# Gates projected beside the scans and stored, and all the memory's keys beside the first convolutions: a hybrid encoder layer

## The chip, the cores and the metric

The kernel runs on one core of a Trainium2 chip. The metric is the device time of one execution in microseconds. The kernel before took 1302.97 us, the median of three runs (1302.38 to 1303.3). All numbers below are from one profiled execution of it.

## The reference, cut to what matters

One layer over 512 tokens of width 1024, in float32:

```python
h = rms_norm(x)
z, xBC, dt_f, dt_b, q, k, v, gates = split(h @ w_in)
xBC = silu(conv5(xBC))                    # centred, depthwise
y = ssd_scan(forward) + ssd_scan(backward) + d_skip * xs   # 4 groups of 8 heads
branch_ssd  = group_rmsnorm(y * silu(z)) @ w_branch_ssd
branch_attn = windowed_attention(rope(q), rope(k), v) @ w_branch_attn
g_ssd, g_attn = sigmoid(gates)            # 1024 columns each
x = x + (g_ssd * branch_ssd + g_attn * branch_attn) @ w_out
x = x + cross_attention(rms_norm(x), rms_norm(mem))    # mem: 256 tokens; keys and values from mem
x = x + swiglu_ffn(rms_norm(x))
return rms_norm(x)
```

The change concerns two projections: the gates of the attention branch (`g_attn`, 8 tiles of 128 columns of `h @ w_in`) and the keys of the memory (8 tiles of 128 columns of `mem_n @ w_kv`).

## The kernel before, in words

Data lie transposed, 128 columns on the partitions and tokens along the free axis, so a projection's result is a tile of 128 x 512 (128 x 256 for the memory). Each matrix product is done in three passes: an operand is split into a high part (`hh`, `whi`) and a low remainder (`hl`, `wlo`), and `mac` (L134 to L141) issues for each of 8 slices hi x hi (L139), hi x lo (L140) and lo x hi (L141): 24 matmuls, accumulated in one PSUM bank of the tag "mm", of which there are three.

A weight tile of 512 KB ("granule") is fetched by SP into `raw` (L121, two buffers), cast by ScalarE into `whi` (L129) and subtracted by VectorE into `wlo` (L130), three buffers each. The program is a list of `steps`, and each granule is loaded LOOK = 2 granules ahead of its step.

The stages: values and keys of the memory and the first norm; the dt step and the first group's convolutions; four group scans; the attention branch; the merge of the two branches; cross-attention; feed-forward. In the first part, up to the attention branch, a planner orders the instructions of each engine by a simulated timeline; the step list gives the priorities. Each engine then works through its own order strictly, waiting where something is late. Later stages are ordered by priority too, so that matmuls of a following step fill in among earlier ones.

A convolution (`conv`, L406 to L417) empties its bank by one ScalarE activation and four VectorE multiply-adds (L414). A group's scan (`group_scan`) has weighing on POOL into `xw` (L495, two buffers), carried states (L503 to L510), decay rows fetched by SP (`rt`), masked on POOL (L537) and exponentiated on ScalarE (L544), added on POOL (L550), multiplied on VectorE (L555), and the inner products on TensorE (L565). Beside a scan the kernel weaves other projections, in an order written by hand in the strings `ONE` and `TWO`: "m" the next group's convolutions, "z" its own z, "o" the output projection of the group before. The first group has no group before it; its "o" slots take five of the eight memory keys. The other three keys are woven with the first group's convolutions (KV1 = 11 of the 16 steps of `kv`; the first eight are values).

A key (`mem_k`, L257 to L262) is scaled by VectorE into an `xw` buffer and stored in DRAM by a DMA that POOL issues; a value (`mem_v`) likewise, from ScalarE. The memory's normalised tiles use the buffers of `vh` and `vl`, which each group's normalised output needs.

In the merge, for each of 8 tiles: `gate_a` projects the gate from `hh`, `hl` and takes a tanh into `ta` (L871, two buffers), then `branch_a` projects the attention output, VectorE multiplies by the gate (L879) and adds the other branch (L880), and the result is split into `mh`, `ml`. The merge's buffers lie where attention's lay, so `ta` and `xr` (x read again, L898) can be written only when attention is through. The gates of the other branch, `gate_s`, are projected in the last scan and in attention.

Of the kernel before, what the change touches and what calls it, by code (L numbers as in the profile page):

```python
# [9 lines left out]
F32 = mybir.dt.float32  # L10
F32R = mybir.dt.float32r
AF = mybir.ActivationFunctionType
# [3 lines left out]
P = 128  # L16
D = 1024
S = 512
KT = D // P
# [21 lines left out]
G_DT, G_K, G_V, G_Q, G_GA, G_SSD, G_GS, G_N = 0, 1, 3, 5, 13, 21, 61, 69  # L41
LOOK = 2
KV0 = 8
G0, G1, TL = 2, 3, 2
KV1 = 11
RB = 3
MB = 3
SPLIT = 1
# [3 lines left out]
HALF = 1  # L52
KVB = 2
LO_POOL = range(0)
HI_DVE = range(79, 89)
ZP = 2
ONE = "mrwomomoo"
TWO = "mzmzm"
LAST = "zezee"
LAG1, LAG2, LAG3 = 1, 2, 5  # L60
# [5 lines left out]
def weave(a, b):  # L66

    key = [((i + 0.5) / len(a), 0, i) for i in range(len(a))] + [((i + 0.5) / len(b), 1, i) for i in range(len(b))]
    return [(a, b)[w][i] for _, w, i in sorted(key)]
# [3 lines left out]
def bidir_hybrid_layer(ctx: ExitStack, tc: tile.TileContext, io, dbg=None):  # L73
    nc = tc.nc
# [9 lines left out]
    dram = ctx.enter_context(tc.tile_pool(name="dram", bufs=1, space=bass.MemoryType.DRAM))  # L84
# [5 lines left out]
    vdr = dram.tile([P, 2, D], F32, tag="vdr", name="vdr")  # L90
    adr = dram.tile([64, S], F32, tag="adr", name="adr")
    edr = dram.tile([64, S], F32, tag="edr", name="edr")

    def bank(tag):
        return ps.tile([P, 512], F32, tag=tag, name=tag, bufs={"mm": 3, "sa": 2, "sb": 3}[tag])
# [20 lines left out]
    def load(spec, i):  # L116
# [7 lines left out]
        for h in range(2 if i < HALF else 1):  # L124
            t = slice(512 * h, 512 * h + 512) if i < HALF else slice(0, n)
            if i in HI_DVE:
                nc.vector.tensor_copy(hi[:, t], raw[:, t])
# [6 lines left out]
    def mac(acc, w, xh, xl, nk=KT, k0=0, w0=0, first=True, last=True):  # L134
        hi, lo = w
        for k in range(nk):
            wh = hi[:, (w0 + k) * P:(w0 + k + 1) * P]
            wl = lo[:, (w0 + k) * P:(w0 + k + 1) * P]
            nc.tensor.matmul(acc, wh, xh[:, k0 + k], start=first and k == 0, stop=False)  # L139
            nc.tensor.matmul(acc, wh, xl[:, k0 + k], start=False, stop=False)  # L140
            nc.tensor.matmul(acc, wl, xh[:, k0 + k], start=False, stop=last and k == nk - 1)  # L141

    def proj(w, xh, xl, n=S):
        acc = bank("mm")
        mac(acc[:, :n], w, xh, xl)
        return acc
# [50 lines left out]
    st = {}  # L197
    pools = {}

    def add(fn, *grans):  # L200
        steps.append((fn, grans))

    def full(src):
        return (src, 1024)
# [60 lines left out]
    def mem_v(hf, k2):  # L265
        def f(w):
            if k2 == 0:
                st["va"] = [bank("mm") for _ in range(2)]
            wh, wl = w
            for c in range(2):  # L270
                o = st["va"][c]
                for j in range(2):
                    k = 2 * k2 + j
                    a, b = st["nh"][:, k, c * P:(c + 1) * P], st["nl"][:, k, c * P:(c + 1) * P]
                    nc.tensor.matmul(o, a, wh[:, j * 512:(j + 1) * 512], start=k == 0, stop=False)
                    nc.tensor.matmul(o, a, wl[:, j * 512:(j + 1) * 512], start=False, stop=False)
                    nc.tensor.matmul(o, b, wh[:, j * 512:(j + 1) * 512], start=False, stop=k == KT - 1)
            if k2 == 3:
                for c in range(2):
                    t = st["sp"].tile([P, S], F32, tag="xw", name="xw", bufs=2)  # L280
                    nc.scalar.activation(t, st["va"][c], AF.Copy, scale=st["mr"][:, c:c + 1])
                    nc.gpsimd.dma_start(vdr[:, c, hf * 512:(hf + 1) * 512], t)
        return f
# [35 lines left out]
    kv = [(mem_v(hf, k2), (full(io["w_xv"][hf, k2]),)) for hf in range(2) for k2 in range(4)]  # L319
# [158 lines left out]
    def group_z(g):  # L478
        def z_step(i):
            def f(w):  # L480
                acc = proj(w, st["hh"], st["hl"])
                zs = st["sp"].tile([P, S], F32, tag="zs", name="zs", bufs=4)
                nc.scalar.activation(zs, acc, AF.Tanh, scale=0.5)
                nc.vector.scalar_tensor_tensor(zs, zs, 1.0, acc, op0=ALU.add, op1=ALU.mult)
                st["zs", g, i] = zs
            return f
        return [(z_step(i), (full(io["w_in"][G_SSD + 10 * g + 6 + i]),)) for i in range(4)]
# [148 lines left out]
    def group_out(g):  # L636
        def f2(q):
            def f(w):
                for j in range(2):
                    m = 2 * q + j  # L640
                    acc = bank("mm")
                    mac(acc, w, st["vh"], st["vl"], nk=4, w0=4 * j)
                    if g == 0:
                        nc.vector.tensor_tensor(bs[:, m], acc, st["vrow"], op=ALU.mult)
                    else:
                        t = st["sp"].tile([P, S], F32, tag="cvt", name="cvt", bufs=1)
                        nc.vector.tensor_tensor(t, acc, st["vrow"], op=ALU.mult)
                        nc.gpsimd.tensor_tensor(bs[:, m], bs[:, m], t, op=ALU.add)
            return f
        return [(f2(q), (full(io["w_bs"][g, q]),)) for q in range(4)]  # L650


    def early_gate(m):
        def f(w):
            if m == 0:
                st["eg"] = st["sp"].tile([P, NCH, S], F32, tag="xk", name="xk", bufs=2)
            acc = proj(w, st["hh"], st["hl"])
            nc.scalar.activation(st["eg"][:, m], acc, AF.Tanh, scale=0.5)
        return f

    def apply_early():
        for m in range(4):
            nc.vector.scalar_tensor_tensor(bs[:, m], st["eg"][:, m], 1.0, bs[:, m], op0=ALU.add, op1=ALU.mult)
# [8 lines left out]
    first, last = group_in(0)  # L672
    add(dt_step, full(io["w_in"][G_DT]))
    steps += weave(first, kv[KV0:KV1])
    for g in range(G):
        z, (more, turn) = group_z(g), group_in(g + 1) if g + 1 < G else ([], [])
        scan1, scan2 = group_scan(g)
        out = group_out(g - 1) if g else kv[KV1:]
        early = [(early_gate(m), (full(io["w_in"][G_GS + m]),)) for m in range(4)] if g == G - 1 else []
        kinds = {"m": list(more), "z": z[ZP:], "o": list(out), "e": early,  # L680
                 "r": [(group_rms, ())] if g else [], "w": [(group_row, ())] if g else []}

        def take(order):
            return [kinds[c].pop(0) for c in order if kinds[c]]

        one = take(ONE if g < G - 1 else ONE + "e")
        if g == 0:
            one += take("o" * len(kinds["o"]))
        two = take(TWO if g < G - 1 else LAST)
        steps += z[:ZP] + last  # L690
        steps += weave(scan1, one)
        steps += weave(scan2, two)
        last = turn
    add(group_rms)
    add(group_row)
    steps += group_out(G - 1)
    add(apply_early)
    closes("sp")

# [150 lines left out]
    win = io["w_in"]  # L850
# [13 lines left out]
    closes("at")  # L864


    def gate_a(m):
        def f(w):
            acc = proj(w, st["hh"], st["hl"])
            t = st["mw"].tile([P, S], F32, tag="ta", name="ta", bufs=2)  # L870
            nc.scalar.activation(t, acc, AF.Tanh, scale=0.5)  # L871
            st["ta", m] = t
        return f

    def branch_a(m):
        def f(w):
            acc = proj(w, st["oh"], st["ol"])
            t, mh, ml = st["ta", m], st["mh"][:, m], st["ml"][:, m]
            nc.vector.scalar_tensor_tensor(t, t, 1.0, acc, op0=ALU.add, op1=ALU.mult)  # L879
            nc.vector.tensor_tensor(t, t, bs[:, m], op=ALU.add)  # L880
            nc.scalar.activation(mh, t, AF.Copy, scale=0.5)
            nc.vector.scalar_tensor_tensor(ml, t, 0.5, mh.bitcast(F32), op0=ALU.mult, op1=ALU.subtract)
        return f
# [22 lines left out]
    opens("mw")  # L906
    add(mw_open)
    for m in range(KT):
        add(gate_a(m), full(win[G_GA + m]))
        add(branch_a(m), full(io["w_ba"][m]))  # L910
    steps += [(mix_out(m), (full(io["w_mo"][m]),)) for m in range(KT)]
    closes("mw")
# [223 lines left out]
    for i, (fn, gr) in enumerate(steps):  # L1136
# [5 lines left out]
        w = ready[taken:taken + len(gr)]  # L1142
# [98 lines left out]
```

## Time and profile before

| | |
|---|---|
| median of three runs | 1302.97 us |
| the profiled execution | 1303.36 us |
| its span | 1301.6 us |
| TensorE (PE) busy | 1253.2 us, 96% |
| VectorE (DVE) busy | 773.0 us, 59% |
| ScalarE (ACT) busy | 565.5 us, 43% |
| GpSimd (POOL) busy | 290.7 us, 22% |
| DMA engines | 143.48 MB, mean 110 GB/s |

Busy times are shares of the span. Matmuls overlap one another, so the busy time of PE counts a matmul from its start to its modelled end. PEld is the load of the stationary operand, which overlaps with matmuls. A name after an arrow in brackets is what an engine's idle time ended with. The granted clock of TensorE is given as a share of 2.4 GHz.

### The profile page before, as it was taken

The numbers are of one execution on the slowest core, as the hardware profiler recorded it, in microseconds if no ns is written. First come the engines' busy times: TensorE is split into PE (matmuls) and PEld (weight loads), VectorE is DVE, ScalarE is ACT, GpSimd is POOL, SyncE is SP. The second block draws the span as 40 slices with busy tenths as digits, with TensorE's granted clock in tenths as the row PEclk, the third lists the DMA queues.
The fourth block names the chain that finished last, engine by engine and source line by source line (L and its number), as shares of the span: only waits on it lengthen the run. The fifth ranks groups of instructions, "written<-read, shape, count | busy, mean of one in ns | idle before, by whom it ended". The sixth has DMA issues, their size and how long they took to land.

```text
span 1301.6 us, 16248 instructions
## 1 busy us (share of the span) xinstructions
PE 1253.2 (96%) x6076; PEld 1011.6 (78%) x6076; DVE 773.0 (59%) x1235; ACT 565.5 (43%) x1062; POOL 290.7 (22%) x250
## 2 busy tenths in 40 slices
PE   7998899999989999999999999999999999999996
PEld 5776588778678688877667888887888888888886
DVE  6785896687777865678873445665444444432323
ACT  6557645365455232358783234444332222222220
POOL 2004722442571733111000002001111111110001
PEclk9999899999999999999999999999999999999998
DMA  7446553454354232321114333322322223233331
GB/s 252 153 138 179 160 166 122 130 157 135 108 152 131 85 120 69 120 98 33 49 34 145 97 99 104 123 65 65 97 94 97 96 94 95 97 97 96 92 98 65
DMA packets 49614, 143.48 MB, mean 110 GB/s; under 512 B 5120, under 2 KB 8576, under 8 KB 49536
## 3 DMA queue, kind: packets, MB, share of 16 engines
q1 hardware_dynamic: 47536, 138.58, 34.5%
q0 software_dynamic: 704, 2.10, 0.4%
q10 hardware_dynamic: 1296, 1.77, 0.4%
q8 instruction: 48, 0.79, 0.3%
q14 instruction: 30, 0.25, 0.1%
HBM read 137.97 MB, written 4.46 MB: 109 GB/s over the span
## 4 chain that ended last, share of the span: by engine, by line
PE 59%; issue 5%; DVE 2%; ACT 2%; POOL 1%; DMA 0%; DVEq 0%; ACTq 0%; POOLq 0%
PE mm L139 18%; PE mm L141 18%; PE mm L140 18%; PE sb L823 1%; PE sb L810 1%; PE sb L997 1%; PE sa L966 1%; POOL rsw L722 1%; PE sa L782 1%; ACT rsw L721 0%; ACT whi L129 0%; PE sa L784 0%; ACT sm L795 0%; PE sb L154 0%; PE sb L172 0%
## 5 line engine op out<-in xcount | busy, mean ns | idle before, releaser
L129 ACT CAST whi<-raw 128x1024 fp32r<-128x1024 f32 (+2 forms) x192 | 199.0, 1036 | 467.6 <-PE mm L140 390.7
L139 PE MATMUL mm<-hh,whi 128*128 128x512 f32 x968 | 382.5, 396 | 5.6 <-DVE cvu L414 2.2
L141 PE MATMUL mm<-hh,wlo 128*128 128x512 f32 x968 | 380.5, 393 | 0.9 <-DVE wlo L130 0.9
L140 PE MATMUL mm<-hl,whi 128*128 128x512 f32 x968 | 380.0, 393 | 0.0
L130 DVE TENSOR_TENSOR wlo<-raw,whi 128x1024 fp32r<-128x1024 f32 (+2 forms) x202 | 250.3, 1239 | 153.8 <-ACT whi L129 144.1
L139 PEld LDWEIGHTS mm<-hh,whi 128*128 128x128 f32 x968 | 182.7, 189 | 47.0 <-issue 5.7
L141 PEld LDWEIGHTS mm<-hh,wlo 128*128 128x128 f32 x968 | 182.6, 189 | 40.2 <-issue 1.8
L140 PEld LDWEIGHTS mm<-hl,whi 128*128 128x128 f32 x968 | 182.8, 189 | 36.8 <-issue 1.0
L544 ACT ACTIVATE rt<-rt,nb 128x128 f32<-128x128 f32 x256 | 78.4, 389 | 61.7 <-POOL rt L537 61.7
L187 POOL TENSOR_TENSOR sq_acc<-sq_acc,sq 128x512 f32<-128x512 f32 x14 | 24.3, 1738 | 262.9 <-ACT sq L186 262.9
L1050 POOL TENSOR_TENSOR fa<-fa,row 128x512 f32<-128x512 f32 x22 | 39.0, 1775 | 192.4 <-ACT fa L1049 192.4
L139 PE MATMUL mm<-vh,whi 128*128 128x512 f32 (+1 forms) x192 | 71.1, 371 | 9.2 <-DVE cvu L414 5.6
L139 PE MATMUL mm<-fh,whi 128*128 128x512 f32 (+1 forms) x198 | 72.6, 367 | 0.0
L140 PE MATMUL mm<-fl,whi 128*128 128x512 f32 (+1 forms) x198 | 72.4, 365 | 0.0
L141 PE MATMUL mm<-fh,wlo 128*128 128x512 f32 (+1 forms) x198 | 72.3, 365 | 0.0
L414 DVE SCALAR_TENSOR_TENSOR cvu<-mm,hcw,cvu 128x510 f32<-128x510 f32 (+1 forms) x96 | 71.1, 743 | 1.3
L141 PE MATMUL mm<-vh,wlo 128*128 128x512 f32 (+1 forms) x192 | 70.5, 367 | 0.0
L140 PE MATMUL mm<-vl,whi 128*128 128x512 f32 (+1 forms) x192 | 68.4, 356 | 0.0
L537 POOL TENSOR_SCALAR_AFFINE_SELECT rt<-rt 128x512 f32<-128x512 f32 x64 | 48.0, 776 | 57.4 <-DMA rt<-adr 55.5
L1052 DVE TENSOR_TENSOR ft<-fa,mm 128x512 f32<-128x512 f32 x22 | 15.1, 688 | 72.9 <-PE mm L141 70.7
L550 POOL TENSOR_TENSOR mt<-rt 128x512 f32<-128x512 f32 x32 | 46.1, 1454 | 19.8 <-PE sa L565 19.8
L139 PEld LDWEIGHTS mm<-vh,whi 128*128 128x128 f32 x192 | 36.6, 190 | 17.8 <-issue 7.3
(230 smaller groups left out, 1941.0 us busy)
## 6 DMA issues: line engine op xcount, KB each, us to landing
raw<-in_w_in SPq DMA_DIRECT2D x69, 512.0 KB, 3.5
raw<-in_w_fi SPq DMA_DIRECT2D x44, 512.0 KB, 3.5
rt<-adr SPq DMA_DIRECT2D x32, 512.0 KB, 5.5
ear<-edr SPq DMA_DIRECT2D x32, 256.0 KB, 4.4
raw<-in_w_bs SPq DMA_DIRECT2D x16, 512.0 KB, 3.5
raw<-in_w_fo SPq DMA_DIRECT2D x16, 512.0 KB, 3.5
raw<-in_w_xk SPq DMA_DIRECT2D x8, 512.0 KB, 3.5
raw<-in_w_ba SPq DMA_DIRECT2D x8, 512.0 KB, 3.5
```

What stands on the lines that cost most here:

```text
L129: nc.scalar.copy(hi[:, t], raw[:, t])
L130: (nc.gpsimd if i in LO_POOL else nc.vector).tensor_tensor(lo[:, t], raw[:, t], hi[:, t].bitcast(F32), op=ALU.subtract)
L139: nc.tensor.matmul(acc, wh, xh[:, k0 + k], start=first and k == 0, stop=False)
L140: nc.tensor.matmul(acc, wh, xl[:, k0 + k], start=False, stop=False)
L141: nc.tensor.matmul(acc, wl, xh[:, k0 + k], start=False, stop=last and k == nk - 1)
L187: eng.tensor_tensor(acc, acc, sq, op=ALU.add)
L414: nc.vector.scalar_tensor_tensor(u[:, b], acc[:, a], w5[j], u[:, b], op0=ALU.mult, op1=ALU.add)
L537: nc.gpsimd.affine_select(out=rt[:, d].rearrange("p (c l) -> p c l", c=NCH), in_=rt[:, d].rearrange("p (c l) -> p c l", c=NCH), pattern=[[ ...
L544: nc.scalar.activation(r, r, AF.Exp, bias=st["nb"][:, c, e0:e0 + 1])
L550: nc.gpsimd.tensor_tensor(mt, st["rt", g, h][:, 0], st["rt", g, h][:, 1], op=ALU.add)
L1050: nc.gpsimd.tensor_tensor(a, a, st["row2"], op=ALU.mult)
L1052: nc.vector.tensor_tensor(t, a, st["fp", 2 * j + 1], op=ALU.mult)
```

## The change

The eight gates of the attention branch are no longer projected in the merge. A new step `early_ga` projects one beside a scan, takes its tanh into an `xw` buffer and stores it in DRAM (`gdr`) by a DMA that POOL issues; in the merge `stored_a` fetches it into `ta` by a DMA on SP. Five gates take the "o" slots of the first group, where the five keys were; the other groups get one each, at a new letter "g" in `ONE`. All eight keys are woven with the first convolutions (KV1 = 16). HI_DVE names granules by number and is moved by the eight granules that now come earlier.

```diff
-KV1 = 11
+KV1 = 16
+GE = (5, 1, 1, 1)
-HI_DVE = range(79, 89)
+HI_DVE = range(87, 97)
-ONE = "mrwomomoo"
+ONE = "mrwomogmoo"
+    gdr = dram.tile([P, KT, S], F32, tag="gdr", name="gdr")
...
+    def early_ga(m):
+        def f(w):
+            acc = proj(w, st["hh"], st["hl"])
+            t = st["sp"].tile([P, S], F32, tag="xw", name="xw", bufs=2)
+            nc.scalar.activation(t, acc, AF.Tanh, scale=0.5)
+            nc.gpsimd.dma_start(gdr[:, m], t)
+        return f
...
     steps += weave(first, kv[KV0:KV1])
+    ega = [(early_ga(m), (full(io["w_in"][G_GA + m]),)) for m in range(sum(GE))]
     for g in range(G):
...
-        out = group_out(g - 1) if g else kv[KV1:]
+        gates, ega = ega[:GE[g]], ega[GE[g]:]
+        out, gates = (group_out(g - 1), gates) if g else (gates, [])
-        kinds = {"m": list(more), "z": z[ZP:], "o": list(out), "e": early,
+        kinds = {"m": list(more), "z": z[ZP:], "o": list(out), "e": early, "g": gates,
...
+    def stored_a(m):
+        def f():
+            st["ta", m] = t = st["mw"].tile([P, S], F32, tag="ta", name="ta", bufs=2)
+            nc.sync.dma_start(t, gdr[:, m])
+        return f
...
     for m in range(KT):
-        add(gate_a(m), full(win[G_GA + m]))
+        if m < sum(GE):
+            add(stored_a(m))
+        else:
+            add(gate_a(m), full(win[G_GA + m]))
         add(branch_a(m), full(io["w_ba"][m]))
```

## Rows read from the trace of the kernel before

**Rows 1.** The page's first part: busy us (share of the span) and instructions.
```profile
PE 1253.2 (96%) x6076; PEld 1011.6 (78%) x6076; DVE 773.0 (59%) x1235; ACT 565.5 (43%) x1062; POOL 290.7 (22%) x250
```

**Rows 2.** Windows: length, busy us of PE, PEld, DVE, ACT, POOL; PEclk; DMA; GB/s.
```profile
36.00:95.00 59.00, 55.04 (x291) 44.90 (x291) 48.74 (x75) 30.28 (x43) 3.42 (x7) 1.00 0.44 139
95.00:165.00 70.00, 59.17 (x314) 46.01 (x313) 46.81 (x54) 47.16 (x123) 39.47 (x42) 0.90 0.60 170
165.00:258.00 93.00, 93.00 (x484) 75.14 (x483) 71.80 (x97) 42.13 (x80) 30.80 (x31) 1.00 0.47 140
258.00:345.00 87.00, 85.59 (x443) 67.64 (x442) 67.56 (x94) 44.53 (x91) 32.65 (x28) 1.00 0.45 135
345.00:446.00 101.00, 92.91 (x480) 73.39 (x481) 78.11 (x95) 53.52 (x122) 56.17 (x51) 1.00 0.45 128
446.00:522.00 76.00, 74.19 (x357) 60.61 (x356) 48.38 (x60) 20.00 (x26) 29.10 (x20) 1.00 0.29 91
...
58.00:72.00 14.00, 11.07 (x62) 9.11 (x62) 13.63 (x21) 6.86 (x11) 0.00 (x0) 1.00 0.47 149
...
640.00:680.00 40.00, 40.00 (x218) 27.87 (x217) 32.00 (x134) 30.02 (x90) 0.00 (x0) 1.00 0.06 22
700.00:760.00 60.00, 60.00 (x266) 49.71 (x265) 24.40 (x29) 17.96 (x23) 0.00 (x0) 1.00 0.31 97
```

**Rows 3.** Timeline of PE, start and length in us: a gate, a branch, a key.
```profile
699.30 0.39 PE L139 MATMUL mm<-hh,whi 128*128 128x512 f32 x1
...
704.74 0.39 PE L139 MATMUL mm<-oh,whi 128*128 128x512 f32 x1
...
119.86 0.28 PE L139 MATMUL mm<-vh,whi 128*128 128x256 f32 x1
...
121.54 0.28 PE L141 MATMUL mm<-vh,wlo 128*128 128x256 f32 x1
```

**Rows 4.** The page's groups (mean ns) and DMA issues (KB, us to landing).
```profile
L130 DVE TENSOR_TENSOR wlo<-raw,whi 128x1024 fp32r<-128x1024 f32 (+2 forms) x202 | 250.3, 1239 | 153.8 <-ACT whi L129 144.1
L129 ACT CAST whi<-raw 128x1024 fp32r<-128x1024 f32 (+2 forms) x192 | 199.0, 1036 | 467.6 <-PE mm L140 390.7
L414 DVE SCALAR_TENSOR_TENSOR cvu<-mm,hcw,cvu 128x510 f32<-128x510 f32 (+1 forms) x96 | 71.1, 743 | 1.3
...
raw<-in_w_ba SPq DMA_DIRECT2D x8, 512.0 KB, 3.5
xr<-in_x SPq DMA_DIRECT2D x4, 512.0 KB, 5.2
vdr<-xw POOLq DMA_DIRECT2D x4, 256.0 KB, 4.7
kdr<-xw POOLq DMA_DIRECT2D x8, 128.0 KB, 2.6
```

**Rows 5.** Timeline at the end of attention: PE's first and last, SP's reload of x.
```profile
655.62 0.40 PE L139 MATMUL mm<-hh,whi 128*128 128x512 f32 x1
...
688.42 0.39 PE L139 MATMUL mm<-oh,whi 128*128 128x512 f32 x1
687.52 1.75 SPq L898 DMA_DIRECT2D xr<-in_x  x4
```

**Rows 6.** Timeline of PE: matmuls that waited, with what ended the wait.
```profile
68.08 0.35 PE L139 MATMUL mm<-vh,whi 128*128 128x256 f32 x1 [2.92 <-DVE cvu L414]
111.23 0.76 PE L139 MATMUL mm<-hh,whi 128*128 128x512 f32 x1 [2.23 <-DVE cvu L414]
148.13 0.80 PE L139 MATMUL mm<-hh,whi 128*128 128x512 f32 x1 [1.73 <-DVE xw L261]
368.57 0.47 PE L139 MATMUL mm<-vh,whi 128*128 128x512 f32 x1 [2.67 <-DVE cvu L414]
```

**Rows 7.** Timeline of VectorE and ScalarE: a key emptied, the first normalised tile.
```profile
147.66 0.41 DVE L261 TENSOR_TENSOR xw<-mm,sq 128x256 f32<-128x256 f32 x1
169.25 0.73 ACT L191 ACTIVATE vh<-vv,vec 128x512 fp32r<-128x512 f32 x1 [0.46 <-PE mm L141]
```

## The prediction, made before the change was run

> **What bounds the kernel now.** I read the page first: TensorE (PE) is busy 1253 us, 96% of the span [rows 1], so some 50 us of plain idle time at most can be won. The windows, stretch by stretch, show where they lie [rows 2]. From 700 us on PE is solid (60.00 of 60), so work taken out there comes straight off the end. The idle is ahead of the attention branch: 4.0 us in the stretch of the first convolutions (55.04 of 59), 10.8 us around the first group's scan (59.17 of 70), none in the next stretch, then 1.4, 8.1 and 1.8 us: 26.1 us from 36 to 522 us. The clock adds to it: around the first scan the mean granted clock is 0.90 where every other stretch has 1.00, which is 14 of 70 us at the 1.2 GHz level instead of 2.4; with PE busy in 59.17/70 of them, 14 / 2 x 0.845 = 5.9 us are lost. PE had idled just before: 2.23 us ahead of 111.23 and 1.73 us ahead of 148.13, where the matmul takes 0.76 and 0.80 us [rows 6].
>
> So the question is not whether PE does less (the change leaves its work as it is) but how much of the gates, moved from a solid stretch to a holey one, falls into holes.
>
> The PE row overstates itself elsewhere too: from 640 to 680 us it is 40.00 of 40 busy while the weight loads, one per matmul, take 27.87 us; at the rate of 700 to 760 (49.71 of 60) they would take 33.1 [rows 2]. The Trainium skill ("Perfetto Trace Analysis", Identifying the Most-Contended Engine) says that matmul busy time is no good measure of the distance to the roofline, and names weight-load time and FLOPs used instead; this trace agrees, with those numbers. By weight loads, the six stretches from 36 to 522 us hold 367.7 us of them, 444 us at the solid rate in 486 us: 42 us of room, an estimate from that page's measure, where idle and clock give 26.1 + 5.9 = 32.0.
>
> **The merge stretch: gates out.** A gate's 24 matmuls start at 699.30 and the branch projection after it at 704.74 [rows 3]: 5.44 us, 8 x 5.44 = 43.5 us, or 0.227 us a matmul. Their weight loads, splits and activations go along; the projections left keep their cadence, with DVE busy 24.4 of 60 us for 11 of them [rows 2], 2.2 us each.
>
> Two things come back. First, filler for the end of attention. Between 655.62 and 688.42, when the last attention output has come, PE did 48 matmuls of this stretch in between (24 of gate 0, 12 each of branch 0 and gate 1) [rows 5]. Now only the first halves of branches, whose heads are done, can be run ahead, 12 matmuls each and, with three "mm" banks, 36. So 12 x 0.227 = 2.7 us go back behind attention. Second, a stored gate comes by DMA on SP, behind the 2 MB of x issued from 687.52 [rows 5] with 5.2 us to landing [rows 4]: at about 696. The three half branches end at 688.4 + 36 x 0.227 = 696.6, and branch 3 needs the bank of branch 0, so the first gate and one DVE operation. I take 1.0 us (0 to 4). From then on, the load of gate m waits on SP until the tile of m-2 is read, within branch m-1, and the weight loads stand behind it. The weight next in line is wanted at least one whole branch and a half later, 8 us, against 3.5 for landing and some 2.3 for the split on ScalarE and DVE [rows 4]: hidden, with 2 us to spare. Sum: -43.5 + 2.7 + 1.0 = -39.8 us.
>
> **The first convolutions: five more keys.** A key's matmuls follow each other at 0.12 us (14 steps from 119.86 to 121.54) [rows 3]: 24 are 2.9 us, 14.4 for five. This stretch is DVE's: its one long PE gap, 2.92 us ahead of 68.08, waits for a convolution on DVE [rows 6], and DVE is busy 13.63 of the 14 us there [rows 2]. A convolution takes 5.4 us of PE and 4.2 of DVE (four multiply-adds at 0.74 and a weight split at 1.24 [rows 4]), and the dt chain comes on top; a key takes 2.9 of PE and 1.7 of DVE (0.41 to empty it [rows 7], 1.24 for the split). Keys lower DVE's share, so I let the 2.9 us vanish and pay the rest. The loads of five more weights are hidden: the DMA engines are at 0.44 there [rows 2]. Bounds: 0 and 4.0.
>
> **The first scan: gates for keys.** Five gates for five keys: 27.2 us in, 14.4 out. Seven PE gaps make up the 10.8 us; two lie before 115 us (3.4 us together, 2.23 of them ahead of 111.23), the last is at 148.13 [rows 6]. The first two wait for the head chain and a convolution on DVE; PE now arrives some 11 us later and DVE only some 8 (five keys), so they should go. The other five (7.4 us) wait for weighted states and products, and at 148.13 for a bank: keys whose matmuls ended at 121.54 kept their banks until DVE could write the shared "xw" buffer at 147.66 [rows 3, 7]. Gates use the same buffers at the same places in the order, so this stays in part; a longer gate fills 2.6 us of it. I take 6.0 of the 10.8, and 2.5 of the 5.9 us of clock. Bounds: 0 and 16.7. One wait leaves: the first normalised tile stood at 169.25 for the last key [rows 7], which read the same buffer; no PE time hung on it.
>
> **The later scans: one gate each.** 16.3 us in. The second group's stretch is full: nothing is absorbed. The third's has 8.1 us, waits for DVE to empty banks (2.67 ahead of 368.57 the longest) [rows 6]; a gate is emptied by ScalarE and gives DVE 5.4 us to catch up: I take 4.5 of it. Of the 1.4 and 1.8 us, 1 each. Bounds 0 and 11.3.
>
> **Sum.** Added 43.5, absorbed 2.9 + 6.0 + 2.5 + 4.5 + 2 = 17.9, so +25.6; with -39.8 that is -14.2 us. The profiled execution took 1303.36 us, 0.4 over the median of 1302.97: **1289 us**.
>
> **Rivals.**
> *All holes fill.* The keys no longer pin the first group's buffers, and gates float freely. Absorbed 32.0: 1303.4 - 39.8 + 43.5 - 32.0 = 1275. For it: the second stretch, with projections woven into its scan, is already solid. Against: the bank waits. By the skill's measure (42 us of room) it would be 1265.
> *Nothing gained in the first scan.* Absorbed 2.9 + 6.5 = 9.4: 1298. For it: a gate put ahead of the weighing delays a PE that works in order, and with it the chain that the later gaps wait for.
> *Slower: the gates' way out jams.* A gate's tanh stands in ScalarE's order, where exponentials and weight casts queue behind it; a key was emptied by DVE. The tanh needs one of two "xw" buffers, and the buffer is free again when its store has landed: 4.7 us for 256 KB, by the memory's values, against 2.6 for a key [rows 4]. If the tanh is put ahead of a buffer's release, five gates over two buffers hold banks 5 x 2.1 / 2 = 5.3 us longer, and the exponentials with them; with 2.9 absorbed alone: 1303.4 - 39.8 + 43.5 - 2.9 + 5.3 = 1309.6. It decides from the point where ScalarE idles on "xw". Against: the order is planned, and the keys were set behind the weighing.
>
> **Chances.** Forecast (1280 to 1296) 0.55; all holes 0.20; nothing in the first scan 0.12; jam 0.13. Within 0.2% (2.6 us), about what a measurement of this kernel can tell from no change, lie only the edges of the last two: same 0.06; slower 0.11; faster 0.83. The range, 1273 to 1305, leaves out the deep end of the second case and most of the jam.
>
> **What would show it.** Right: the merge stretch about 40 us shorter with PE solid in it; the first convolutions longer by 10 to 13 us with no gap near 68; PE idle in the first scan down to about 5 us and its clock above 0.90; a gate inside the third group's gaps. Wrong: PE waiting for a "ta" DMA or a late weight after attention, ScalarE idle ahead of a tanh, or as much PE idle in the first scan as before.

## The result and the profile after

The changed kernel takes 1291.32 us (median of 4 runs, 1290.67 to 1294.08) against 1303.13 (4 runs, 1302.38 to 1303.97) for the kernel before on the same chip: a ratio of 0.9912, with 0.9899 to 0.9925 as its 95% interval. It is faster by 11.8 us where 14.2 were forecast; 1291.3 lies inside the forecast's own band (1280 to 1296). The profiled execution took 1290.67 us, its span is 1288.9.

The page's first part (engine, busy us, share of the span, instructions) shows what [rows 1] shows of before: the same 6076 matmuls, 2.6 us less of PE time.

```profile
PE 1250.6 (97%) x6076; PEld 1013.1 (79%) x6076; DVE 765.2 (59%) x1235; ACT 565.0 (44%) x1062; POOL 295.7 (23%) x258
```

To find where the time went I cut both traces at the same events: the first inner product of the first scan, the statistics that close each of the four groups, the last attention product, the first projection of the merged stream, the end. These are the windows of the changed kernel (columns as in [rows 2]):

```profile
37.10:115.20 78.10, 73.97 (x437) 63.93 (x435) 54.99 (x84) 43.15 (x73) 10.32 (x17) 1.00 0.56 164
115.20:236.30 121.10, 120.99 (x589) 96.39 (x588) 87.13 (x110) 70.04 (x154) 49.31 (x53) 0.99 0.56 164
...
236.30:343.70 107.40, 105.55 (x529) 84.61 (x529) 78.67 (x104) 53.66 (x114) 38.66 (x38) 0.98 0.48 135
343.70:446.00 102.30, 96.19 (x489) 77.88 (x488) 73.97 (x97) 50.41 (x109) 49.46 (x42) 0.97 0.44 132
446.00:529.70 83.70, 83.70 (x426) 66.06 (x426) 53.58 (x67) 27.46 (x48) 39.33 (x30) 1.00 0.35 104
...
714.60:752.20 37.60, 36.35 (x158) 29.22 (x157) 22.69 (x29) 12.26 (x15) 0.00 (x0) 1.00 0.61 209
752.20:1288.90 536.70, 526.16 (x2459) 438.59 (x2458) 232.13 (x330) 170.55 (x241) 72.78 (x47) 0.99 0.29 93
```

And the kernel before, cut at the same events:

```profile
37.10:106.50 69.40, 65.44 (x339) 53.32 (x337) 49.61 (x76) 39.47 (x71) 8.95 (x13) 1.00 0.53 150
106.50:224.80 118.30, 107.47 (x567) 86.24 (x566) 93.18 (x114) 67.06 (x146) 49.37 (x51) 0.94 0.51 157
...
224.80:324.90 100.10, 98.94 (x507) 78.89 (x506) 75.32 (x103) 51.98 (x113) 38.54 (x37) 1.00 0.47 137
324.90:422.10 97.20, 89.98 (x469) 72.02 (x469) 75.81 (x97) 49.02 (x108) 46.99 (x41) 1.00 0.46 130
422.10:501.60 79.50, 78.07 (x398) 60.99 (x397) 53.62 (x65) 25.38 (x45) 38.27 (x29) 1.00 0.32 100
...
686.90:764.60 77.70, 77.70 (x343) 63.94 (x342) 31.00 (x36) 23.61 (x31) 0.00 (x0) 1.00 0.38 122
764.60:1301.60 537.00, 526.14 (x2459) 438.59 (x2457) 232.21 (x330) 170.58 (x241) 72.72 (x47) 0.99 0.29 93
```

Read the lengths downwards: +8.7 up to the first inner product, +2.8 in the first scan, +7.3, +5.1 and +4.2 in the later groups (one gate of 5.44 us each), -40.1 between attention and the merged projections, -0.3 behind. With small shifts in between this is the 12.7 us by which the span shrank. The first scan went from 10.83 us of PE idle (118.30 - 107.47) to 0.11 and from a granted clock of 0.94 to 0.99.

The longest waits of PE that are left before and behind attention, from its timeline (start, length, engine, line, operation; in brackets the wait and what ended it):

```profile
114.59 0.47 PE L141 MATMUL mm<-hh,whi 128*128 128x512 f32 x1 [3.48 <-DVE xw L263]
...
279.09 0.61 PE L141 MATMUL mm<-vh,whi 128*128 128x512 f32 x1 [1.85 <-DVE x L646]
...
374.75 1.85 PE L567 MATMUL sa<-mt,xk 128*64 128x128 f32 x14 [2.63 <-DVE mt L557]
...
397.76 0.63 PE L472 MATMUL sb<-cst,xs 128*128 128x128 f32 x4 [2.99 <-DVE xs L419]
...
715.85 0.96 PE L141 MATMUL mm<-oh,whi 128*128 128x512 f32 x3 [0.68 <-ACT oh L840]
724.92 0.47 PE L141 MATMUL mm<-oh,whi 128*128 128x512 f32 x1 [0.57 <-DVE ta L898]
```

The waits at 68.08, 111.23 and 148.13 of [rows 6] are gone. In their place stands the one at 114.59: the next projection has no bank, because the last key is not emptied yet. (That projection is the second of the group's own z, which ScalarE empties into `zs` at 128.32; the gates come later.) VectorE's and ScalarE's timelines show it:

```profile
113.42 0.69 DVE L557 TENSOR_TENSOR mt<-mt,cb 128x512 f32<-128x512 f32 x1 [13.21 <-POOL mt L552]
114.03 0.41 DVE L263 TENSOR_TENSOR xw<-mm,sq 128x256 f32<-128x256 f32 x1
...
128.32 0.59 ACT L485 ACTIVATE zs<-mm 128x512 f32<-128x512 f32 x1
```

The key's evacuation is queued on DVE behind the first masked product, for which DVE stood 13.21 us idle. The key's last matmul had ended at 105.7; emptying it took 0.41 us.

### The profile page after: what moved, and what is told of

Its sections match the earlier page's. It is cut to its first block, busy times and chain, and to the rows that moved or that the text cites. A ratio compares the mean times of both kernels' runs of the same rounds, so it can differ in the third digit from the quotient of the medians.

```text
span 1288.9 us, 16269 instructions
## 1 busy us (share of the span) xinstructions
PE 1250.6 (97%) x6076; PEld 1013.1 (79%) x6076; DVE 765.2 (59%) x1235; ACT 565.0 (44%) x1062; POOL 295.7 (23%) x258
## 3 DMA queue, kind: packets, MB, share of 16 engines
q10 hardware_dynamic: 1296, 1.77, 0.4%
## 4 chain that ended last, share of the span: by engine, by line
PE 78%; issue 6%; DMA 5%; ACT 4%; DVE 3%; POOL 3%; SPq 0%; ACTq 0%; DVEq 0%; POOLq 0%
PE mm L141 23%; PE mm L142 22%; PE mm L143 22%; DMA rt<-adr 4%; PE sb L505 2%; ACT rt L546 1%; PE sb L579 1%; PE sb L836 1%; POOL rsw L735 1%; PE sa L567 1%; PE sb L823 1%; PE sb L1019 1%; ACT whi L131 1%; POOL mt L552 1%; DVE wlo L132 1%
## 5 line engine op out<-in xcount | busy, mean ns | idle before, releaser
L132 DVE TENSOR_TENSOR wlo<-raw,whi 128x1024 fp32r<-128x1024 f32 (+2 forms) x202 | 255.3, 1264 | 145.7 <-ACT whi L131 135.5
L552 POOL TENSOR_TENSOR mt<-rt 128x512 f32<-128x512 f32 x32 | 50.3, 1585 | 19.1 <-PE sa L567 19.0
L141 PE MATMUL mm<-oh,whi 128*128 128x512 f32 x128 | 49.6, 392 | 1.2 <-ACT oh L840 0.7
```

Source lines behind the costliest of these rows:

```text
L132: (nc.gpsimd if i in LO_POOL else nc.vector).tensor_tensor(lo[:, t], raw[:, t], hi[:, t].bitcast(F32), op=ALU.subtract)
L552: nc.gpsimd.tensor_tensor(mt, st["rt", g, h][:, 0], st["rt", g, h][:, 1], op=ALU.add)
```

## The experiments

Ten further kernels, each timed beside the kernel before. Each expectation calls A the account I held when it was written and sets a rival against it. The kernels differ from the changed one by the lines shown, except where it says otherwise; where the number of early gates differs from eight, the list of weight splits given to VectorE (HI_DVE) is shifted by as many. Times are medians, the brackets behind a ratio its 95% interval. The runs were made on three chips, on which the kernel before took 1303.53, 1303.79 and 1304.16 us, so runs from different chips are best compared by their ratios. An edit also makes the planner order the engines anew.

**Do the three later gates pay?** All five early gates stay in the first scan, the other three go back to the merge stretch.

```
-GE = (5, 1, 1, 1)
+GE = (5, 0, 0, 0)
```

> Gates 5 to 7 are projected in the merge as before; only the five gates of the first group are moved. Theory A, as the marks of the two traces read: each later scan pays its gate in full (7.3, 5.1 and 4.2 us for 5.4 each), so taking the three back changes nothing: 1291 us, within 2. Rival, the prediction's term for the later scans: 6.5 us of their holes were filled, so taking the gates back costs that: 1298 us.

1289.88 us, ratio 0.9898 [0.988, 0.9917], as A had it; after stands at 0.9912 [0.9899, 0.9925], so no difference can be told. Its windows for groups two to four and for the merge stretch:

```profile
235.40:334.40 99.00, 98.89 (x506) 78.84 (x505) 76.72 (x103) 51.95 (x112) 37.81 (x37) 1.00 0.45 139
334.40:431.30 96.90, 91.52 (x469) 73.23 (x469) 76.15 (x97) 49.20 (x108) 48.05 (x41) 0.98 0.44 131
431.30:510.80 79.50, 78.11 (x398) 60.99 (x397) 53.54 (x65) 25.38 (x45) 38.21 (x29) 1.00 0.31 100
697.20:751.00 53.80, 52.74 (x231) 42.78 (x230) 26.30 (x32) 16.83 (x22) 0.00 (x0) 1.00 0.47 162
```

The groups are back at before's lengths within 1.1 us, and the merge stretch is 16.2 us longer than in after. There the three gates had cost 7.3 + 5.1 + 4.2 = 16.6 in the groups: moved for nothing. The third group keeps its idle time with the gate in it (6.1 of 102.30) or not (5.4 of 96.90).

**How many gates fill the first scan?** Three, and all eight.

```
-GE = (5, 1, 1, 1)
+GE = (3, 0, 0, 0)     # three_first
+GE = (8, 0, 0, 0)     # eight_first
```

> Only three gates, all in the first scan; five stay in the merge. Theory A: the first scan and the convolutions have holes of about 16 us and the first gates fall into them for nothing: 3 x 5.4 us leave the merge at a price near 1 us, and attention keeps its filler, 1288 us. Rival, each gate fills a like share (15.7 of 27.2 for five): three absorb 9.4 of 16.3, 1294 to 1297 us.

> All eight gates in the first scan, none in the later ones. Theory A: its holes are full after five, three more pay 5.4 us each as they do in the later scans: 1291 us, within 2. Rival, the scan goes on absorbing about 3.1 us a gate: 1282 us.

Eight: 1292.61, ratio 0.9917 [0.9902, 0.9932], as A had it. Its first group ends 19.3 us after that of five gates (254.7 against 235.4) for 16.3 us of gates: from five on, the first scan is full too. Three: 1298.37, ratio 0.9963 [0.9947, 0.9979]: A fell, and the rival's range ends 1.4 us below the median, within the interval (1296.6 to 1300.8 us). The nine executions of this kernel reach from 1295.79 to 1302.79 us; the one with the profile, 1302.04, has the lowest granted clock of them, 0.987 over the span; three of the four shortest have 0.992. In it the first group ends at 235.1, where five gates end. PE's timeline has two waits, where first_only has one of 2.91 us:

```profile
117.27 0.76 PE L141 MATMUL mm<-hh,whi 128*128 128x512 f32 x1 [3.92 <-DVE xw L263]
...
181.87 1.12 PE L472 MATMUL sb<-cst,xs 128*128 128x128 f32 x4 [3.37 <-DVE xs L419]
```

and the windows around them a granted clock of 0.66:

```profile
115.00:125.00 10.00, 7.73 (x22) 5.58 (x23) 6.70 (x9) 6.01 (x18) 6.23 (x6) 0.66 0.79 228
180.00:190.00 10.00, 8.13 (x25) 6.17 (x26) 8.61 (x9) 5.68 (x14) 6.03 (x5) 0.66 0.52 155
...
37.10:235.10 198.00, 189.67 (x984) 154.66 (x982) 143.07 (x194) 112.15 (x225) 59.66 (x67) 0.97 0.53 161
```

Each of the two holds 0.34 x 2 x 10 = 6.8 us at 1.2 GHz, a loss of 3.4 us of PE's full rate. Idle up to the first group's end is 8.3 us, against 5.1 with five gates (198.30 - 193.22), where the granted clock is 1.00: 3.2 us of idle and 6.8 of clock make 10.0 us, most of what two gates take (10.9). So this execution loses by two waits and by the clock behind them. Of the others there is no profile: they take up to 6.3 us less, yet the shortest (1295.79) still takes longer than every execution of first_only (1288.64 to 1293.79). Why the order with three gates makes DVE late at 181.87 stays open.

**What do the keys alone bring?** No gate is moved, the five keys are.

```
-GE = (5, 1, 1, 1)
+GE = (0, 0, 0, 0)
```

> All keys beside the first convolutions, no gate moved: eight gates in the merge. Theory A, the first scan's length is set by its head chain and PE has spare time in it: the keys' 14 us appear in the convolutions and little of it is given back: 1308 to 1313 us. Rival, the keys that held banks made the scan's holes, and without them it shortens by what they took: 1298 to 1303 us.

1298.07, ratio 0.9962 [0.995, 0.9975]: 5 us faster, by the rival; A, which had the moved keys as a loss without the gates, fell. The profile is of the fastest of six executions, 1295.83 us, 7.5 below the profiled one of before. Its window from the first convolutions to the first group's end:

```profile
37.10:215.20 178.10, 170.48 (x909) 137.76 (x908) 135.66 (x189) 105.47 (x216) 58.55 (x64) 0.99 0.55 163
```

The same work is done 9.6 us earlier than before: idle is 7.6 us where it was 14.8 (69.40 + 118.30 - 65.44 - 107.47), the clock 0.99 where it was 0.96. (Of that, 1 us is lost again in the second group and 1.7 in attention.)

**Why do the keys cost so much where they were?** In the kernel before itself, the keys are emptied into unused halves of another tile instead of the shared "xw".

```
-            t = st["sp"].tile([P, S], F32, tag="xw", name="xw", bufs=2)[:, :MEM]
+            t = x1[:, 4, MEM * (m % 2):MEM * (m % 2) + MEM]
```

> The kernel before with one edit: a key is emptied into a free part of x1 and not into one of the two xw buffers that the weighing uses. Theory A, the keys' banks were held until an xw buffer came free, and that made the first scan's holes: the wait of 1.73 us ahead of 148 goes and most of the 5 us that moving the keys gave come without moving them, 1296 to 1299 us. Rival, the keys' place in the order and DVE's share of work made the holes: no change, 1302 to 1304 us.

1299.58, ratio 0.9968 [0.9955, 0.9982], at the upper end of A's range and clear of the rival's. On VectorE's timeline the fourth key, emptied at 147.66 before [rows 7], is emptied 18.9 us earlier, and on PE's the wait of [rows 6] at 148.13 is gone; what is left there is

```profile
128.73 0.42 DVE L261 TENSOR_TENSOR x<-mm,sq 128x256 f32<-128x256 f32 x1
```

```profile
129.29 0.36 PE L139 MATMUL mm<-vh,whi 128*128 128x256 f32 x1 [1.59 <-DVE x L261]
137.20 0.47 PE L139 MATMUL mm<-hh,whi 128*128 128x512 f32 x1 [2.28 <-DVE cvu L414]
```

So a bank was held by a finished product that had no SBUF buffer to go to: 4.2 us of the kernel. In the kernel before, all three "mm" banks were taken from 137.5, when the fifth key's matmuls ended, to 148.1: by the fourth key (emptied at 147.66), by the fifth, and by a convolution still waiting for its last multiply-add. VectorE's timeline there:

```profile
148.00 0.73 DVE L414 SCALAR_TENSOR_TENSOR cvu<-mm,hcw,cvu 128x510 f32<-128x510 f32 x1
...
154.27 0.42 DVE L261 TENSOR_TENSOR xw<-mm,sq 128x256 f32<-128x256 f32 x1 [0.84 <-DMA kdr<-xw]
```

**Do the gates gain without the keys' move?** The keys stay in the first scan, with five gates behind them; then the same with the buffers of both taken from the other tile.

```
-KV1 = 16
+KV1 = 11
-        out, gates = (group_out(g - 1), gates) if g else (gates, [])
+        out, gates = (group_out(g - 1), gates) if g else (kv[KV1:] + gates, [])
-GE = (5, 1, 1, 1)
+GE = (5, 0, 0, 0)
# five_only_x1 also: the key's t as above, and for the gates
-            t = st["sp"].tile([P, S], F32, tag="xw", name="xw", bufs=2)
+            t = x1[:, m % 4]
```

> The kernel before with five gates added to the first scan behind its five keys, three left in the merge: gates alone, keys unmoved. Theory A, with the keys' banks held the scan cannot take the gates in, they pay 5.4 us each and the merge gives back 4.8 each: 1303 to 1307 us. Rival, the two halves of the change add up (gates alone gave 8.2 us once the keys were gone): 1293 to 1297 us.

> Keys at their old places, five gates added to the first scan, but keys and gates emptied into free parts of x1, not into xw. Theory A, the held banks alone kept the scan from taking the gates in: with them free it takes them as well as with the keys moved away, 1289 to 1294 us. Rival, the keys' place counts by itself, since in the first convolutions they fill PE's wait for DVE (2.9 us) and in the scan they stand with ten projections too many: 1297 to 1302 us.

five_only: 1305.35, ratio 1.0008 [0.9996, 1.002], as A had it: nothing gained. five_only_x1: 1297.89, ratio 0.9956 [0.9942, 0.997], by the rival. In five_only the bank wait is still on PE's timeline

```profile
147.19 0.80 PE L141 MATMUL mm<-hh,whi 128*128 128x512 f32 x1 [2.07 <-DVE xw L263]
```

and the windows up to the first group's end, for five_only and then for five_only_x1, show the idle time shrink from 13.9 to 9.8 us:

```profile
37.10:250.70 213.60, 199.74 (x1026) 164.11 (x1025) 146.02 (x193) 113.65 (x225) 61.70 (x69) 0.97 0.51 154
```

```profile
37.10:244.30 207.20, 197.45 (x1023) 162.37 (x1022) 144.69 (x193) 114.01 (x226) 57.99 (x69) 0.98 0.52 158
```

**Does the shared buffer still cost anything after the change?** The five-gate kernel with the other buffers.

```
-GE = (5, 1, 1, 1)
+GE = (5, 0, 0, 0)
# and t of the keys and of the gates as in five_only_x1
```

> The run with five gates in the first scan and three in the merge, with keys and gates both emptied into free parts of x1 and not into xw. Theory A, with the keys gone xw holds nothing up that matters: the same within 1.5 us, 1290. Rival, the gates' banks are still held by xw: 1283 to 1287 us, and PE's waits near 114 and 135 us gone.

1289.05, ratio 0.9885 [0.9868, 0.9901], against 0.9898 [0.988, 0.9917] with "xw": the same. Its window and its wait:

```profile
37.10:236.00 198.90, 194.68 (x1026) 160.57 (x1025) 141.00 (x193) 113.27 (x225) 60.05 (x69) 0.99 0.55 165
```

```profile
115.26 0.47 PE L141 MATMUL mm<-hh,whi 128*128 128x512 f32 x1 [3.92 <-DVE x L263]
```

Idle is 4.2 us, and the last key waits as long in a buffer of its own: once the keys are out of the scan it is DVE's queue, not the buffer, that holds it. From five_only_x1 to this kernel only the keys' place differs: 8.8 us of median, 8.3 at the first group's end. PE's waits for convolutions at 67.08, 111.14 and 135.65 us of five_only_x1 (3.05, 2.23 and 2.28 us) are gone here, and its idle time falls from 9.8 to 4.2.

**Can that last wait be had?** The keys are woven into the first four steps only, so that the last is emptied before DVE turns to the products.

```
-    steps += weave(first, kv[KV0:KV1])
+    steps += weave(first[:4], kv[KV0:KV1]) + first[4:]
# with GE = (5, 0, 0, 0)
```

> The run with five gates in the first scan and three in the merge, with the eight keys woven with the first four convolutions only, so that the last two convolutions stand behind all keys. Theory A, PE's one long wait (2.9 us near 114) is the last key, which stands on DVE behind the first product of the scan, late by the decay rows: it goes, 1286 to 1288 us. Rival, a convolution then stands in that place on DVE, or DVE falls behind with two convolutions in a row as in the kernel before: 1290 to 1293 us.

1291.64, ratio 0.9906 [0.9889, 0.9924], no better than first_only, as the rival said. The wait for the key goes, and on PE's timeline others come:

```profile
112.20 0.41 PE L567 MATMUL sa<-mt,xk 128*64 128x128 f32 x2 [0.51 <-DVE mt L557]
113.84 0.66 PE L567 MATMUL sa<-mt,xk 128*64 128x128 f32 x8 [1.24 <-DVE mt L557]
116.95 0.77 PE L141 MATMUL mm<-hh,whi 128*128 128x512 f32 x1 [2.45 <-DVE cvu L416]
```

**What does the lost filler at the end of attention cost?** In first_own_buf the stored gates are 3 to 7 instead of 0 to 4; gates 0 to 2 are projected in the merge stretch, where their matmuls can run ahead beside attention's last heads.

```
-    ega = [(early_ga(m), (full(io["w_in"][G_GA + m]),)) for m in range(sum(GE))]
+    ega = [(early_ga(m), (full(io["w_in"][G_GA + m]),)) for m in range(KT - sum(GE), KT)]
-        if m < sum(GE):
+        if m >= KT - sum(GE):
```

> Five gates in the first scan, three in the merge, own buffers, as the run of 1289 us; but the three that stay are now gates 0 to 2, and gates 3 to 7 are the stored ones. Theory A, the prediction's terms for the merge (12 matmuls of filler, 2.7 us, and a late first gate, up to 1 us): from the last attention product to the first merged projection 50 to 51 us and not 53.7, 1286 us. Rival, attention's end waits for its own chain whatever PE has to fill: 53 to 54 us, 1289 us.

1287.32 (1286.22 to 1288.43), ratio 0.9872 [0.9857, 0.9886]: the fastest kernel of the study. The merge stretch, from the last attention product to the first merged projection, here and then in first_own_buf:

```profile
698.30:748.80 50.50, 50.50 (x222) 41.40 (x221) 24.87 (x31) 15.89 (x20) 0.00 (x0) 1.00 0.46 160
```

```profile
698.30:752.00 53.70, 52.65 (x230) 42.74 (x229) 26.28 (x32) 16.82 (x21) 0.00 (x0) 1.00 0.46 162
```

3.2 us shorter and solid again, as A had it; the waits for "oh" and "ta" of the changed kernel have no counterpart. The medians differ by 1.7 us and their intervals overlap, so the stretch shows the gain and the whole time only leans to it. Against after (0.9912 [0.9899, 0.9925]) the intervals are apart: the three edits together, late gates, own buffers and filler, are worth 4 to 5 us (4.0 by the medians, 5.2 by the ratios).

## Why the prediction was right, and which of its terms were not

**The question was the right one.** The gates left a solid stretch (before: 77.70 of 77.70) and entered a holey one, and the gain is what the holes took in: 43.5 us went in, attention starts 28.1 us later (25.6 forecast), so 15.4 were absorbed where the sum had 17.9. By place the sum was wrong in three terms that nearly cancel, so that the total came within 2.4 us of the forecast is in part luck.

**First convolutions: 2.9 forecast, nothing measured.** The gap at 68.08 went, as predicted. But idle up to the first inner product is 4.13 us against 3.96: the last key, emptied late in DVE's queue, put a wait of 3.48 us there instead. (Of the 10 to 13 us by which this stretch was to grow, 8.7 show; it holds 98 matmul records more, not 120, so some 22 slid behind the first product.)

**First scan: 6.0 of idle and 2.5 of clock forecast, 10.7 and some 5 measured.** Idle fell from 10.83 to 0.11; the clock share from (1 - 0.94) x 118.3 x 0.91 = 6.4 to about 1.2. With the term above, 11.4 were forecast and 15.7 came; the change has its 3.48 us wait just ahead of the cut, before had its 2.23 [rows 6] just behind it, so the two terms are best read together. The step that failed is the one behind "gates use the same buffers at the same places in the order, so this stays in part": a bank held is not yet PE time lost. The holding did stay in part. The first gate's matmuls end at 133.8, and ScalarE empties it at 149.91, 16 us later. The waits of the first two gates, 0.29 and 1.04 us, end when a matmul has read "xw" (L505):

```profile
133.42 0.39 PE L143 MATMUL mm<-hh,wlo 128*128 128x512 f32 x1
...
149.91 0.60 ACT L668 ACTIVATE xw<-mm 128x512 f32<-128x512 f32 x1 [0.29 <-PE sb L505]
151.55 0.60 ACT L668 ACTIVATE xw<-mm 128x512 f32<-128x512 f32 x1 [1.04 <-PE sb L505]
```

What did not stay is the idle time: PE always found another bank or other work (0.11 us idle). With buffers of their own, in first_own_buf, the first gate is emptied 0.9 us after its matmuls end (134.6), and the kernel is no faster than first_only:

```profile
135.50 0.59 ACT L668 ACTIVATE x<-mm 128x512 f32<-128x512 f32 x1
```

ScalarE idle ahead of a tanh was a sign of the rival in which the tanh jams. It is there, 1.3 us of it, but it cost PE nothing, and that rival falls.

before_keys_x1, five_only and five_only_x1 show the mechanism from its other side: with the keys in place the gates gain nothing; a buffer of its own for each is worth 4.2 us without the gates and some 7 with them; the rest is the keys' place beside the first convolutions. The Trainium skill ("Perfetto Trace Analysis", Optimization Strategy) says that consistent bubbles on the engine that should be saturated can mean too little SBUF or PSUM for the next tile. In this case a buffer was missing too, with those numbers, though the gap did not repeat: a single bank held for 26 us (121.54 to 147.66, [rows 3, 7]) shows as one wait of 1.73 us [rows 6], and the buffer was worth more than that.

The room that the prediction read from weight-load time (42 us) was not there: PE is solid in the changed first scan (120.99 of 121.10) with loads at 96.39 / 121.1 = 0.80 of the time, where the estimate took 0.83 as solid.

**The later groups: 6.5 forecast to be absorbed, nothing measured.** 16.6 us paid for 16.3. The reason given, that a gate emptied by ScalarE lets DVE catch up, failed: the third group's idle is 6.1 us after 7.2, and the granted clock in the second and third falls from 1.00 to 0.98 and 0.97, behind the waits at 279.09, 374.75 and 397.76. The clock won in the first scan was lost there again: the mean over the span is 0.991 in both profiles. first_only confirms that these gates were moved for nothing: one that stands in the third group leaves its idle time as it is.

**The merge stretch: -39.8 forecast, -40.1 measured.** The 2.7 us of lost filler, put back in the sum, is real: a gate taken out is worth 23.9 / 5 = 4.8 us (77.7 to 53.8), not 5.44, and filler_kept returns 3.2. The wait for the first stored gate, 1.0 forecast, is 0.57; it was named as a sign of being wrong, but its size is within the term.

**The rivals.** "All holes fill" holds for the first scan alone; over all groups 15.4 us were absorbed, not 32.0. "Nothing gained in the first scan" is refuted by that scan's 0.11 us of idle. (The jam rival's terms add up to 1309.5, not 1309.6.) "All holes fill" named the keys' hold on buffers, but none of them priced it: the keys' move, which I costed as a price to be hidden, is a gain of its own, 5 us of median, beside some 8 that the five gates add to it and nothing for the other three.

## What to carry to other kernels

When work is exchanged in a stretch, look first at what leaves it: a finished product that waits in PSUM for a shared SBUF buffer can stop TensorE, and its removal can be worth as much as the work moved in. Count the banks that are left, though: here a gate held one for 16 us and cost nothing. Count filler only for holes whose cause the filler does not share: a stretch that waits for an engine late by its own chain keeps its idle time, and the moved work is paid in full. What is taken out of the front of a solid stretch may have been covering the end of the one before; take it from the back.

## What was not expected of the hardware

The price of a short PE wait is not its length. In the three-gate kernel waits of 3.92 and 3.37 us were each followed by a granted clock of 0.66 over 10 us, 6.8 us at 1.2 GHz. In four kernels with five gates in the first scan the wait for the last key, near 115 us, was 2.91 us (first_only), 3.48 (the changed kernel), 3.92 (first_own_buf) and 3.14 (filler_kept):

```profile
113.76 0.47 PE L141 MATMUL mm<-hh,whi 128*128 128x512 f32 x1 [2.91 <-DVE xw L263]
...
115.59 0.77 PE L141 MATMUL mm<-hh,whi 128*128 128x512 f32 x1 [3.14 <-DVE x L263]
```

and these are their windows around it, in the same order:

```profile
115.00:125.00 10.00, 10.00 (x45) 8.25 (x45) 6.67 (x9) 6.06 (x17) 6.37 (x6) 1.00 0.87 237
115.00:125.00 10.00, 10.00 (x39) 7.81 (x38) 6.67 (x9) 5.75 (x14) 6.02 (x7) 0.83 0.87 252
115.00:125.00 10.00, 9.74 (x35) 7.51 (x36) 6.66 (x10) 5.78 (x16) 5.85 (x7) 0.83 0.95 258
115.00:125.00 10.00, 9.41 (x28) 6.95 (x29) 6.82 (x10) 5.87 (x15) 5.58 (x7) 0.66 0.93 256
```

The granted clock was 1.00, 0.83, 0.83 and 0.66: the longest of the four waits did not cost the most. The kernel before shows it with shorter ones: 1.73 us ahead of 148.13 [rows 6] went with 0.66 from 145 to 155 us. Nor does one kernel always pay the same: the nine executions of three_first have mean granted clocks from 0.987 to 0.992 and differ by 7 us. What decides is open.
